# Hybrid SSD and latent-attention layer on one core: the last four FFN tiles of the down projection in parts of 352 and 224 tokens instead of 320 and 256, and the end of the issue order left to the scheduler

## The chip, the core and the metric

One NeuronCore of a Trainium2 chip. The time is the device time of one execution in microseconds; before the change three runs gave 637.97, 638.06 and 638.47, with a median of 638.06. A difference is told as a part of that median.

The engines are TensorE (PE in the profile, with its weight loads as PEld), VectorE (DVE), ScalarE (ACT), GpSimd (POOL) and SyncE (SP). Each runs its own list of instructions in order and waits on semaphores for the others. SBUF is the memory on the chip, and PSUM holds what TensorE sums, in banks of 512 f32 columns.

## What is computed

One layer for 576 tokens: 512 of a new stream and 64 of a running one. Two head groups (state space and latent attention) are mixed, and a dense SwiGLU FFN follows. The change lies in the last two lines of this part of the reference:

```python
x = x + concatenate([y_ssd, o], axis=-1) @ p['w_out']
hf = rmsnorm(x, p['norm_ffn'])
x = x + (silu(hf @ p['w_gate']) * (hf @ p['w_up'])) @ p['w_down']     # 1024 -> 2816 -> 1024
y = rmsnorm(x, norm_final)                                           # over the 1024 channels of each token
```

All inputs and outputs are f32.

## The kernel before

Channels lie on the 128 partitions and tokens along the columns, so `x` is 8 tiles of 128 x 576 (`x2[0]` to `x2[7]`, held in two buffers that the profile shows as `x2_0` for tiles 0 to 3 and `x2_1` for 4 to 7). The hidden layer of the FFN has 22 tiles of 128 channels. The first 18 go through the gate, up and down projections by a scheme of 2x2 block products with 288 columns each. Tiles 18 to 21, the last four, are gated in the same way (L894 holds the matmuls of the gate and up products, `finish` the silu and product), and their down projection is done in plain form at the very end: that is where the change is.

Products are made with three matmuls in place of one f32 matmul. Each operand is split into a rounded part and the rest, both held in the rounded f32 form (fp32r); `wh`, `wl` and the two halves of `pr18` to `pr21` are these parts, and high x high, high x low and low x high are summed in PSUM. `split_weights` (L127, L128) and `split_scaled` (L157, L159) make them. Each of the 8 output tiles needs 4 x 3 = 12 such matmuls for a part of the tokens (`down_half`, L1104).

The tokens of this last product are cut in two parts (`parts`, L1139). For part 0, tile by tile:

- 12 matmuls into a PSUM bank (`ps_l0_t`), then `add` (L1146, VectorE) adds the bank to `x2[t]`.
- ScalarE squares the sum (L1186) and multiplies the tile by its gain (`gain`, L1150); GpSimd and VectorE add the squares up (L1191, L1194, L1196).
- One f32 matmul with a matrix of ones (L1232) sums the squares over the partitions, and `norm_steps` (L186 to L193) makes the reciprocal root from it on ScalarE and VectorE, by a logarithm, an exponential and one correcting step. L1238 copies the result to SBUF for GpSimd.
- `outs` multiplies the eight tiles by it: six on VectorE (five in L1161, tile 7 in L1157), two on GpSimd (L1159). `send` (L1167) sends them to memory in pairs, on SyncE's queue.

Part 1 goes the same way, with the matmuls in `ps_l1_t`, the squares in L1240, their sums in L1245 and L1247, and its norm packed into half as many columns (L1206). Tile 7 is summed on top of a copy of `x2[7]` in PSUM (L1229). The norm is spread to all partitions by four small matmuls (L1266), and ScalarE copies it for GpSimd (L1267). The tiles are sent one by one, on SyncE's and ScalarE's queues in turn (`SENDS`, L1164). Seven matmuls (L1260), of which nothing is read, stand between L1206 and L1266.

What sets the order: the kernel is written with a scheduler that places the instructions of each engine from a simulated timeline, and `ISSUE` (L1324) is a table that overrides it. For each engine it lists the places of its instructions, counted in the order in which the program makes them, and `issue_in_order` ties each to the next one listed. An instruction that no list names is placed by the scheduler.

```python
    parts = [slice(0, 320), slice(320, T)]
    def lbank(tag, name, i):
        return bank(tag, name)[:, : parts[i].stop - parts[i].start]
    ORDERS = ((0, 4, 1, 5, 2, 3, 6, 7), (0, 2, 3, 1, 4, 5, 6, 7))
    OUTS = {3: (0, 1), 4: (2, 3, 4), 5: (5, 6), 6: (7,)}
```

Of the kernel before, what the change touches and what calls it, by code (L numbers as in the profile page):

```python
# [23 lines left out]
T = TP + TS  # L24
# [32 lines left out]
def hybrid_layer_kernel(ctx: ExitStack, tc: tile.TileContext, a, o):  # L57
# [35 lines left out]
    def tmp(name, w=T):  # L93
        return placed(tpool, [P, UPW], F32, "t", name)[:, :w]
# [1041 lines left out]

    R3 = R1
    sql = tmp("sq_last")
    parts = [slice(0, 320), slice(320, T)]  # L1139

    def lbank(tag, name, i):
        return bank(tag, name)[:, : parts[i].stop - parts[i].start]
# [298 lines left out]
4022 4019 4023-4025 4046 3969 4047-4048 4034 3989 4026-4027 4049-4050 4028 4020 3990 4029 4051 4035 4052 4036-4039  # L1441
4030-4031 3970 4032 4040-4041 4053-4054 4033 4055-4056 4042 4070 4043-4045 4021 4057-4059 4071 4060 3991 4061 4082
4062 4072-4075 4063-4065 4083 4066-4069 4076 4084 4077-4081 4085 4094-4098 4086 4099 4087 4118-4119 4100-4101 4130
4102 4106-4107 4103 4108 4131 4104 4109 4120 4088 4110-4111 4089-4090 4121 4132-4134 4091 4105 4092-4093 4187 4135
4112-4116 4136 4117 4178 4137 4122-4127 4142 4138 4128 4143-4147 4139-4140 4179 4129 4196 4148-4151 4180 4152 4181
4153 4205 4182 4154 4183 4188 4155-4156 4206 4141 4197 4157-4158 4189 4166 4159-4160 4167 4161 4190 4168-4169 4162
4238 4170 4191 4198 4163 4192 4164 4193 4171-4172 4199 4165 4184 4200 4226 4173 4201 4174-4177 4239 4194 4227 4207
4185 4208 4195 4202 4228 4203 4229 4298 4209 4230 4240-4241 4231 4186 4210 4242 4204 4211 4262 4243 4212 4214 4232
4220 4213 4217 4223 4215-4216 4233 4221 4244 4222 4218 4245 4224 4263 4250 4225 4251 4246 4252-4255 4247 4256 4219
4234 4257 4235 4248 4236 4299 4249 4264-4265 4258-4259 4237 4260-4261 4266-4267 4274-4275 4268-4269 4276 4286-4287  # L1450
4270 4288 4271-4273 4300 4289 4277-4278 4290-4294 4335 4279 4295 4323 4280 4296 4281-4282 4301 4310 4283-4285
4302-4303 4311 4304 4312 4305 4336 4297 4337 4306 4313-4315 4307-4308 4347 4338 4324-4326 4309 4327 4339-4341 4328
4316-4317 4329 4348-4349 4330 4350 4318-4321 4331 4351 4342 4332 4352 4333 4322 4353 4334 4354 4343-4346 4359
4355-4358 4360-4382 4384-4387 4383
""",
    "DVE": """
48 1 0 2-4 7 5-6 10 9 8 11 13 12 15 14 16-17 19 30 18 20 23 22 49 21 24 58 25 85 26-29 31-33 35 67 36 34 106 37 68-69
# [26 lines left out]
825 831 834 824 832 860 853 835 842 836 850 859 849 843-844 851 847 845 861 846 838 837 848 852 854 862 839 863 881  # L1484
856 866 858 855 857 864-865 868 871 885 877 867 872 878 882 874 880 873 883 876 879 890 886 891 897 889 907 875 884
888 903 909 887 910 898-899 904 911 900 892 901 919 906 915 908 912 893 914 913 869 905 920-921 923 870 922 917 894
918 924-925 916 895 928 902 927 937 926 929 896 938 932 931 939 930 933-934 940 935-936 941 943-944 942 947 945-946
949 948 950-954 956 955 958-959 957 961 963-964 967-968 971 960 962 965 969 966 970 972-978 980 979
""",
    "ACT": """  # L1490
0-5 8 6-7 11 10 9 13 12 16 14-15 19 17-18 21 20 24 23 40 22 44 25-26 52 27-31 56 32-36 50 48 41 49 60 42-43 45-46 51
# [17 lines left out]
568-569 566 564 561 567 565 571 570 572 577 574 576 575 573 578 580 579 589 582 586 588 581 587 592 590 597 585 583  # L1509
591 584 594 602-603 595 599 596 600 605 598 601 604 606 610-611 609 608 593 612 607 613 630 614 619 616 625 615 624  # L1510
621 617-618 622 626 623 620 627-629 632 631 637 633-636 640 638-639 643 645 648 646 651 654 644 649 647 656 641 650
657 655 659 658 663 660 642 661 664-665 652 666 662 674 667 669 653 675 670 668 677 676 671-673 682-685 678 680 679
688 686 690 687 689 692 697-699 695 693 700 681 701 696 691 711 703 705 707 709-710 712-715 694 706 702 704 708
716-718 720 719
""",
    "POOL": """
0-3 7 18 28 4 8 5 9 6 10 26-27 11 29 12-17 20-22 19 23-25 31 30 32-42 53 55 57 59 54 56 58 60 43-52 61-73 75 74 76-77
79 78 80-85 87 86 88-89 91 90 92-93 95 94 96-106 108-109 107 111 110
""",
    "SP": """  # L1520
11-14 16 15 18 17 19-20 22 21 25 24 39 23 37 26 40 33 38 41-43 34 44 32 45 81 46-48 57 64 79 59 58 56 62 61 65 63 60
83 70 74 67 69 68 71 78 80 88 73 75 72 66 89 77 76 82 86 90-92 87 93 100 103 101-102 104-105 109-118 120 119 122-123
121 124-130 132 131 134 133 136 135 138 137 139-144 146 145 148 147 149-150 152 151 154 153 155-156 158 157 160 159
161-169 171-172 170 174-176 173 177-178 180 179
""",
}

# [98 lines left out]
```

## Time and profile before

| what | value |
|---|---|
| median of three runs | 638.06 us |
| the profiled execution: its time / its span | 637.72 us / 635.8 us |
| PE busy in the span | 625.6 us (98%) |
| DVE, ACT, POOL busy | 552.1, 390.6, 71.6 us |
| granted TensorE clock | 0.996 |
| matmuls of L1104 with 320 columns (records, mean length) | 96, 309 ns |
| matmuls of L1104 with 256 columns | 64 at 286 ns, 32 at 282 ns |
| first part's four sends | 320 KB each, landing after 2.6 us (median) |
| second part's eight sends | 128 KB each, landing after 2.1 us (median) |

The span is the time from the first to the last instruction of the profiled execution; its own time is 1.9 us longer, and the runs' median is 0.34 us above it. A matmul's length in the profile is modelled and longer than its step, since the next one starts before it ends: what a matmul costs in a row of them is the distance from start to start. A row of the timeline has the start, the time to the last one's end, the engine, line, operation, operands and the count of those merged. A plain f32 matmul leaves two records. A row of busy time by stretches has, for each engine, the busy time and the number of instructions, then the granted clock, the DMA engines' share and GB/s.

### The profile page before, as it was taken

The page shows a single profiled execution, that of the slowest core. Times are in us where ns is not written, and L with a number is a line of the kernel's source. Part 1 is how long each engine was busy: PE and PEld are TensorE (multiplying, and loading weights), DVE is VectorE, ACT ScalarE, POOL GpSimd, SP SyncE. Part 2 cuts the span into 40 slices and gives each one's busy share as a digit, 9 for nine tenths or more (in the row PEclk, how much of TensorE's full clock was granted, in tenths as well). Part 3 has the DMA queues.
Part 4 walks back from the last instruction along what each step waited for, and adds up shares of the span by engine and source line. Part 5 has one row for each costly group of instructions (what it writes and reads, how often), then busy time and mean ns, then how long its engine had stood idle before and what let it go on. Part 6 is the DMA issues. An engine that isn't in the chain of part 4 may idle for free.

```text
span 635.8 us, 11941 instructions
## 1 busy us (share of the span) xinstructions
PE 625.6 (98%) x4631; PEld 597.7 (94%) x4631; DVE 552.1 (87%) x981; ACT 390.6 (61%) x752; POOL 71.6 (11%) x111
## 2 busy tenths in 40 slices
PE   9999999999999999999999999999999999999995
PEld 9899999985887899999999999999999999999994
DVE  6999996899867599999998997889888998999764
ACT  7655425789766479955656555656564566635464
POOL 1322122001010000000012002100111011100023
PEclk9999999999999999999999999999999999999998
DMA  9521184314131132232177436551756254733004
GB/s 309 209 59 71 35 210 152 114 30 147 72 112 35 54 133 80 85 116 67 34 185 178 120 100 145 141 136 60 187 131 163 68 162 117 164 106 134 1 1 149
DMA packets 31560, 72.66 MB, mean 114 GB/s; under 512 B 3706, under 2 KB 11400, under 8 KB 31248
## 3 DMA queue, kind: packets, MB, share of 16 engines
q1 hardware_dynamic: 25360, 60.77, 29.6%
q0 software_dynamic: 5424, 10.57, 9.3%
q8 instruction: 36, 0.59, 0.4%
q10 hardware_dynamic: 720, 0.57, 0.3%
q14 instruction: 20, 0.16, 0.1%
HBM read 58.03 MB, written 3.30 MB: 96 GB/s over the span
## 4 chain that ended last, share of the span: by engine, by line
PE 49%; issue 1%; POOL 1%; POOLq 0%; DVE 0%; ACT 0%
PE ps_x L894 17%; PE ps_dx L1034 9%; PE ps_z L894 9%; PE ps_dz L1034 5%; PE ps_y L894 4%; PE ps_l L1104 3%; PE ps_dy L1034 2%; POOL ss L1247 0%; POOL x L1159 0%; POOLq L1613 0%; PE ps_n L1232 0%; DVE x L1146 0%; ACT sq L1240 0%; POOLq L1159 0%
## 5 line engine op out<-in xcount | busy, mean ns | idle before, releaser
L894 PE MATMUL ps_x<-xop,wh_gu_S 128*128 128x288 f32 x504 | 126.3, 295 | 0.0
L894 PEld LDWEIGHTS ps_x<-xop,wh_gu_S 128*128 128x128 f32 x504 | 88.2, 188 | 0.7 <-ACT u L963 0.2
L894 PE MATMUL ps_x<-xop,wl_gu_S 128*128 128x288 f32 x252 | 73.3, 295 | 0.0
L894 PE MATMUL ps_z<-xop,gu_a 128*128 128x288 f32 x252 | 61.7, 295 | 0.0
L127 ACT CAST wh_gu_S<-gu 128x1024 fp32r<-128x1024 f32 x44 | 46.2, 1053 | 14.8 <-PE ps_y L894 4.2
L128 DVE TENSOR_TENSOR wl_gu_S<-gu,wh_gu_S 128x1024 fp32r<-128x1024 f32 x44 | 52.9, 1219 | 0.8 <-ACT wh_gu_S L127 0.5
L894 PEld LDWEIGHTS ps_x<-xop,wl_gu_S 128*128 128x128 f32 x252 | 47.1, 188 | 0.0
L1047 POOL DMA_DIRECT2D x<-db x16 | 14.9, 930 | 279.2 <-ACT db L1040 249.1
L143 PE MATMUL ps_in<-xs,wh_in 128*128 128x288 f32 x256 | 45.4, 298 | 0.0
L894 PE MATMUL ps_y<-xop,wh_gu_A 128*128 128x288 f32 x168 | 44.9, 295 | 0.0
L894 PEld LDWEIGHTS ps_z<-xop,gu_a 128*128 128x128 f32 x252 | 43.5, 188 | 0.0
L894 PE MATMUL ps_z<-xop,wh_gu_S 128*128 128x288 f32 x168 | 43.4, 295 | 0.0
L894 PE MATMUL ps_x<-xop,wh_gu_A 128*128 128x288 f32 x168 | 42.7, 295 | 0.0
L143 PEld LDWEIGHTS ps_in<-xs,wh_in 128*128 128x128 f32 x256 | 37.8, 189 | 0.2
L127 ACT CAST wh_gu_A<-gu 128x1024 fp32r<-128x1024 f32 x22 | 23.1, 1051 | 23.5 <-PE ps_x L894 16.1
L894 PEld LDWEIGHTS ps_y<-xop,wh_gu_A 128*128 128x128 f32 x168 | 30.1, 188 | 0.1
L128 DVE TENSOR_TENSOR wl_gu_A<-gu,wh_gu_A 128x1024 fp32r<-128x1024 f32 x22 | 26.8, 1220 | 3.3 <-ACT wh_gu_A L127 1.8
L894 PEld LDWEIGHTS ps_z<-xop,wh_gu_S 128*128 128x128 f32 x168 | 29.7, 188 | 0.0
L894 PEld LDWEIGHTS ps_x<-xop,wh_gu_A 128*128 128x128 f32 x168 | 29.5, 188 | 0.0
L465 PE MATMUL ps_o<-cat_y,wh_out 128*128 128x288 f32 x128 | 29.0, 312 | 0.0
L143 PE MATMUL ps_in<-xs,wl_in 128*128 128x288 f32 x128 | 27.5, 296 | 0.0
L465 PE MATMUL ps_o<-cat_o,wh_out 128*128 128x288 f32 x128 | 27.4, 297 | 0.0
(597 smaller groups left out, 2002.0 us busy)
## 6 DMA issues: line engine op xcount, KB each, us to landing
gu<-in_w_gu SPq DMA_DIRECT2D x44, 512.0 KB, 4.8
db<-in_w_down SPq DMA_DIRECT2D x16, 512.0 KB, 4.4
x<-db POOLq DMA_DIRECT2D x16, 288.0 KB, 6.6
x<-dc POOLq DMA_DIRECT2D x16, 288.0 KB, 4.3
wr_in<-in_w_in SPq DMA_DIRECT2D x8, 512.0 KB, 5.8
wr_out<-in_w_out SPq DMA_DIRECT2D x8, 512.0 KB, 3.3
cumb<-cumD SPq DMA_DIRECT2D x5, 512.0 KB, 4.9
x<-in_xT SPq DMA_DIRECT2D x2, 1152.0 KB, 5.6
```

The costliest lines, as they stand in the source:

```text
L127: act.copy(hi, raw)
L128: dve.tensor_tensor(lo, raw, hi.bitcast(F32), ALU.subtract)
L143: pe.matmul(ps[:m, hf, :n], w, x[:, hf * n : (hf + 1) * n], start=start and k == 0 and i == 0, stop=stop and k == last and i == 2,)
L465: pe.matmul(ps[:, :n], w, x[:, cols], start=not onto and k == 0 and i == 0, stop=onto or (k == len(terms) - 1 and i == 2), skip_group_chec ...
L894: pe.matmul(ps, p, q, start=not onto and first and kp == kps[0] and j == 0, stop=onto or (last and kp == kps[-1] and j == 2), skip_group_c ...
L1034: pe.matmul(ps, l, r, start=not onto and k == 0 and j == 0, stop=onto or (k == n - 1 and j == 2), skip_group_check=onto,)
L1047: pool.dma_start(x2[t], v, accum_op=ALU.add)
L1104: pe.matmul(ps, w, x[:, cols], start=first and not onto and k == 0 and i == 0, stop=onto or (last and k == len(terms) - 1 and i == 2), ski ...
```

## The change

The first part takes 352 tokens and the second 224. Everything that is cut by `parts` changes its width with it: the matmuls, sums, squares, norms, outputs and sends of the end. The number of instructions on each engine stays the same.

The second half of the change removes the end of each engine's list in `ISSUE`. The lists now stop at PE's place 4177, DVE's 940, ACT's 673, POOL's 100 and SP's 170, so that the last product, both norms and the sends are placed by the scheduler.

```diff
@@ -1136,7 +1136,7 @@
     sql = tmp("sq_last")
-    parts = [slice(0, 320), slice(320, T)]
+    parts = [slice(0, 352), slice(352, T)]
@@ -1441,17 +1441,9 @@
-4102 4106-4107 4103 4108 4131 4104 4109 4120 4088 4110-4111 4089-4090 4121 4132-4134 4091 4105 4092-4093 4187 4135
-4112-4116 4136 4117 4178 4137 4122-4127 4142 4138 4128 4143-4147 4139-4140 4179 4129 4196 4148-4151 4180 4152 4181
...
-4355-4358 4360-4382 4384-4387 4383
+4102 4106-4107 4103 4108 4131 4104 4109 4120 4088 4110-4111 4089-4090 4121 4132-4134 4091 4105 4092-4093 4135
+4112-4116 4136 4117 4137 4122-4127 4142 4138 4128 4143-4147 4139-4140 4129 4148-4156 4141 4157-4158 4166 4159-4160
+4167 4161 4168-4169 4162 4170 4163-4164 4171-4172 4165 4173-4177
 """,
     "DVE": """
...
-918 924-925 916 895 928 902 927 937 926 929 896 938 932 931 939 930 933-934 940 935-936 941 943-944 942 947 945-946
-949 948 950-954 956 955 958-959 957 961 963-964 967-968 971 960 962 965 969 966 970 972-978 980 979
+918 924-925 916 895 928 902 927 937 926 929 896 938 932 931 939 930 933-934 940 935-936
...
     "SP": """
...
-161-169 171-172 170 174-176 173 177-178 180 179
+161-169 171-172 170
```

PE, the place of the first part's norm sum (L1232), before. `ps_l1_2` is the bank of part 1, tile 2; `wh_dl1` and `wl_dl1` are the two parts of a weight tile.

```order
L1104 MATMUL ps_l1_2_7540<-pr19_7021,wh_dl1_7340 128x256
L1232 MATMUL ps_n3_0_7499<-ss3_3201,ones_86 128x320
L1104 MATMUL ps_l1_0_7504<-pr21_7328,wh_dl0_7334 128x256 x2
L1104 MATMUL ps_l1_0_7504<-pr21_7328,wl_dl0_7335 128x256
L1104 MATMUL ps_l1_2_7540<-pr19_7021,wh_dl1_7340 128x256
L1104 MATMUL ps_l1_2_7540<-pr19_7021,wl_dl1_7341 128x256
L1104 MATMUL ps_l1_3_7566<-pr18_6833,wh_dl1_7340 128x256
```

And now:

```order
L1104 MATMUL ps_l1_5_7608<-pr21_7328,wh_dl2_7346 128x224 x2
L1232 MATMUL ps_n3_0_7499<-ss3_3201,ones_86 128x352
L1104 MATMUL ps_l1_5_7608<-pr21_7328,wl_dl2_7347 128x224
L1104 MATMUL ps_l1_6_7629<-pr18_6833,wh_dl3_7352 128x224 x2
L1104 MATMUL ps_l1_6_7629<-pr18_6833,wl_dl3_7353 128x224
L1104 MATMUL ps_l1_6_7629<-pr19_7021,wh_dl3_7352 128x224 x2
L1104 MATMUL ps_l1_6_7629<-pr19_7021,wl_dl3_7353 128x224
L1104 MATMUL ps_l1_6_7629<-pr20_7245,wh_dl3_7352 128x224 x2
L1104 MATMUL ps_l1_6_7629<-pr20_7245,wl_dl3_7353 128x224
L1104 MATMUL ps_l1_6_7629<-pr21_7328,wh_dl3_7352 128x224 x2
L1104 MATMUL ps_l1_6_7629<-pr21_7328,wl_dl3_7353 128x224
```

L1232 moved from among the matmuls of part 1's first tiles to the last matmul of its tile 5. Behind it come that one, the 12 of tile 6 shown and 12 of tile 7 in the same form, then L1206.

DVE, the second norm's first step (L187 of `ps_n3_1`), before. `nr_v` and `nr_u` are the norm's working tiles, `Rp` its packed result, `sq` the squares, and `ps_r3_0` the spread result.

```order
L1157 SCALAR_TENSOR_TENSOR x2_1_2055<-x2_1_2055,par_81,ps_n3_0_7499 128x320
L1146 TENSOR_TENSOR x2_0_2053<-ps_l1_3_7566,x2_0_2053 128x256
L1146 TENSOR_TENSOR x2_1_2055<-ps_l1_4_7586,x2_1_2055 128x256
L1146 TENSOR_TENSOR x2_1_2055<-ps_l1_5_7608,x2_1_2055 128x256
L1146 TENSOR_TENSOR x2_1_2055<-ps_l1_6_7629,x2_1_2055 128x256
L1245 TENSOR_TENSOR sq_7600<-sq_7600,sq_7622 128x256
L1245 TENSOR_TENSOR sq_7600<-sq_7600,sq_7643 128x256
L187 TENSOR_SCALAR nr_v_7673<-ps_n3_1_7500 128x128
L192 TENSOR_TENSOR nr_u_7674<-nr_u_7674,nr_v_7673 128x128
```

And now:

```order
L1146 TENSOR_TENSOR x2_1_2055<-ps_l1_6_7629,x2_1_2055 128x224
L192 TENSOR_TENSOR nr_u_7503<-nr_u_7503,nr_v_7502 128x352
L193 SCALAR_TENSOR_TENSOR ps_n3_0_7499<-nr_u_7503,nr_y_7501 128x352
L1245 TENSOR_TENSOR sq_7600<-sq_7600,sq_7643 128x224
L1161 TENSOR_TENSOR x2_1_2055<-x2_1_2055,ps_n3_0_7499 128x352 x2
L1161 TENSOR_TENSOR x2_0_2053<-x2_0_2053,ps_n3_0_7499 128x352 x2
L1161 TENSOR_TENSOR x2_1_2055<-x2_1_2055,ps_n3_0_7499 128x352
L1157 SCALAR_TENSOR_TENSOR x2_1_2055<-x2_1_2055,par_81,ps_n3_0_7499 128x352
L187 TENSOR_SCALAR nr_v_7673<-ps_n3_1_7500 128x112
L192 TENSOR_TENSOR nr_u_7674<-nr_u_7674,nr_v_7673 128x112
```

The first part's last norm steps and its six outputs stood ahead of the sums of part 1's tiles 3 to 6; now they stand behind these sums, directly ahead of the second norm.

ACT, from the first norm to the end, now:

```order
L188 ACTIVATE nr_y_7501<-nr_y_7501 128x352
L1240 ACTIVATE sq_7622<-x2_1_2055 128x224
L189 ACTIVATE nr_u_7503<-nr_y_7501 128x352
L1150 ACTIVATE x2_1_2055<-x2_1_2055,par_81 128x224
L1240 ACTIVATE sq_7643<-x2_1_2055 128x224
L1150 ACTIVATE x2_1_2055<-x2_1_2055,par_81 128x224
L1238 COPY R1_99<-ps_n3_0_7499 128x352
L1240 ACTIVATE sq_7663<-ps_l1_7_7649 128x224
L186 ACTIVATE nr_y_7672<-ps_n3_1_7500 128x112
L188 ACTIVATE nr_y_7672<-nr_y_7672 128x112
L189 ACTIVATE nr_u_7674<-nr_y_7672 128x112
L1267 COPY R1_99<-ps_r3_1_7690 128x224
```

A square (L1240) now stands between L188 and L189 of the first norm, and the copy L1238 ahead of the last square. The five L1150 that stood between L189 of the second norm and L1267 have moved ahead of it.

More of the change, by code (lines that the diff above doesn't have):

```diff
@@ L1443 @@
 4062 4072-4075 4063-4065 4083 4066-4069 4076 4084 4077-4081 4085 4094-4098 4086 4099 4087 4118-4119 4100-4101 4130
-4102 4106-4107 4103 4108 4131 4104 4109 4120 4088 4110-4111 4089-4090 4121 4132-4134 4091 4105 4092-4093 4187 4135
-4112-4116 4136 4117 4178 4137 4122-4127 4142 4138 4128 4143-4147 4139-4140 4179 4129 4196 4148-4151 4180 4152 4181
[L1446 to L1453, printed above, removed]
-4355-4358 4360-4382 4384-4387 4383
+4102 4106-4107 4103 4108 4131 4104 4109 4120 4088 4110-4111 4089-4090 4121 4132-4134 4091 4105 4092-4093 4135
+4112-4116 4136 4117 4137 4122-4127 4142 4138 4128 4143-4147 4139-4140 4129 4148-4156 4141 4157-4158 4166 4159-4160
+4167 4161 4168-4169 4162 4170 4163-4164 4171-4172 4165 4173-4177
 """,
@@ L1511 @@
 621 617-618 622 626 623 620 627-629 632 631 637 633-636 640 638-639 643 645 648 646 651 654 644 649 647 656 641 650
-657 655 659 658 663 660 642 661 664-665 652 666 662 674 667 669 653 675 670 668 677 676 671-673 682-685 678 680 679
-688 686 690 687 689 692 697-699 695 693 700 681 701 696 691 711 703 705 707 709-710 712-715 694 706 702 704 708
-716-718 720 719
+657 655 659 658 663 660 642 661 664-665 652 666 662 674 667 669 653 675 670 668 677 676 671-673
 """,
@@ L1517 @@
 0-3 7 18 28 4 8 5 9 6 10 26-27 11 29 12-17 20-22 19 23-25 31 30 32-42 53 55 57 59 54 56 58 60 43-52 61-73 75 74 76-77
-79 78 80-85 87 86 88-89 91 90 92-93 95 94 96-106 108-109 107 111 110
+79 78 80-85 87 86 88-89 91 90 92-93 95 94 96-100
 """,
```

## The prediction

> **What bounds the kernel now.** I read the page first (share of each engine, then the chain that ended last), then the busy time by stretches of the end, then the timeline of that end.
>
> ```profile
> span 635.8 us, 11941 instructions
> PE 625.6 (98%) x4631; PEld 597.7 (94%) x4631; DVE 552.1 (87%) x981; ACT 390.6 (61%) x752; POOL 71.6 (11%) x111
> PE 49%; issue 1%; POOL 1%; POOLq 0%; DVE 0%; ACT 0%
> ```
>
> TensorE (PE) is busy for 98% of the span, and what else ends the chain is about 1% each. So there are two ways for an edit of the end to cost time: more TensorE time, or a longer stretch behind the last matmul, where the other engines normalise and send.
>
> ```profile
> core 0: us, PE busy (x) PEld busy (x) DVE busy (x) ACT busy (x) POOL busy (x), PEclk, DMA share, GB/s
> 615.40:620.00 4.60, 4.60 (x38) 4.44 (x37) 3.07 (x8) 3.19 (x8) 1.45 (x2) 1.00 0.01 4
> 620.00:624.50 4.50, 4.50 (x41) 4.37 (x39) 4.15 (x11) 3.19 (x9) 3.46 (x5) 1.00 0.74 255
> 624.50:628.00 3.50, 3.26 (x31) 2.77 (x31) 0.99 (x4) 2.84 (x9) 0.00 (x0) 1.00 0.13 46
> 628.00:632.00 4.00, 0.63 (x6) 0.44 (x4) 2.14 (x6) 0.82 (x3) 1.41 (x2) 0.90 0.68 222
> ```
>
> Up to 624.5 TensorE has no gap, and its clock is granted in full (1.00). From 624.5 to 625.9 the second part's norm starts, and in 624.5:628 VectorE (DVE) is nearly idle (0.99 of 3.50): whatever it had to do for the first part lies behind it. DMA is idle there too (0.13), and is then used for the second part's results alone. These two reserves are what the change touches.
>
> **TensorE's own time.** The change keeps the number of matmuls: 96 of 320 columns become 96 of 352, and 96 of 256 become 96 of 224. The price of one is the step from start to start.
>
> ```profile
> 606.53 0.60 PE L1104 MATMUL ps_l<-pr,wh_dl 128*128 128x320 f32 x3
> 606.97 0.31 PE L1104 MATMUL ps_l<-pr,wl_dl 128*128 128x320 f32 x1
> ...
> 624.04 0.40 PE L1104 MATMUL ps_l<-pr,wh_dl 128*128 128x256 f32 x2
> 624.28 0.28 PE L1104 MATMUL ps_l<-pr,wl_dl 128*128 128x256 f32 x1
> 624.49 0.33 PE L1206 MATMUL ps_n<-ss,ones 128*64 128x128 f32 x2
> ```
>
> Three of 320 columns take 606.97 - 606.53 = 0.44, so 0.147 each; two of 256 take 0.24, so 0.120. That is 0.42 ns a column, 0.107 for 256, and 0.013 on top of either. On this line 352 columns cost 0.147 + 0.013 = 0.160 and 224 cost 0.120 - 0.013 = 0.107. Sum of a pair: 0.267 before, 0.267 after; 96 pairs change nothing.
>
> But no matmul of this rounded form (fp32r) has under 256 columns in the trace, so 0.107 is an extrapolation, and I bound it. Below: a matmul with hardly any columns, whose step is its weight load.
>
> ```profile
> 123.04 1.00 PE L595 MATMUL ps_g<-ysq,ones 128*128 128x64 f32 x8
> 123.87 1.08 PE L571 MATMUL ps_s<-xw,bt 128*128 128x256 f32 x4
> ```
>
> Eight records, each with a 128x128 weight load, step over 0.83, 0.104 each: that floor lies just under 0.107. Above: the plain f32 form, which leaves two records for one instruction.
>
> ```profile
> 615.39 0.78 PE L1232 MATMUL ps_n<-ss,ones 128*128 128x320 f32 x2
> 615.77 0.64 PE L1104 MATMUL ps_l<-pr,wh_dl 128*128 128x256 f32 x2
> 616.25 0.28 PE L1104 MATMUL ps_l<-pr,wl_dl 128*128 128x256 f32 x1
> ```
>
> From 615.39 to 616.25 run one L1232 and two 256-column matmuls, so L1232 took 0.86 - 0.24 = 0.62 for 320 columns; 224 at that rate are 0.434. Between 0.104 and 0.434 I take 0.107, since 224 is only 32 columns past a row that lies on the line; the upper end becomes a rival. If the 13 ns that each step has over its columns stay on top of the weight load, a narrow one costs 0.120 as the 256-column one does, and TensorE loses 96 x 0.013 = 1.3; I keep that inside the forecast's range.
>
> A rule bears on this. The Trainium skill (TensorE: Matmul & The Clock Gate, "LDWEIGHTS (loading the stationary operand)") gives a weight load as its columns over 1.2 GHz, 107 ns for 128. By that floor the 224-column matmul is bound by its weights rather than by its columns, and anything narrower would gain nothing; the sum here would stay the same, and the row's 0.104 agrees with it.
>
> No wait enters TensorE's stream, by the new order and these prices: the narrowest cover is at the silu of the last FFN tile.
>
> ```profile
> 602.41 0.69 ACT L941 ACTIVATE g<-g 128x576 f32<-128x576 f32 x1 [4.44 <-DVE g L983]
> 603.42 0.75 DVE L942 TENSOR_TENSOR u<-u,g 128x576 f32<-128x576 f32 x1
> 604.21 0.69 ACT L157 ACTIVATE pr<-u 128x576 fp32r<-128x576 f32 x1 [1.11 <-DVE u L942]
> 604.93 0.76 DVE L159 TENSOR_TENSOR pr<-u,pr 128x576 fp32r<-128x576 f32 x1 [0.75 <-ACT pr L157]
> ```
>
> `pr21` is there about 4 us after the last gate/up matmul (L983, which waits for that, starts at 601.92; L159 ends at 605.69). The new order puts 38 wide matmuls and 2 narrow ones between it and the first that reads `pr21`: 38 x 0.160 + 2 x 0.107 = 6.3. Without that cover the price would be at most those 4 us.
>
> **The end: where the loss comes from.** The first part's norm (L1232, then L186 to L193) and its eight outputs now stand late. Before:
>
> ```profile
> 616.27 0.44 ACT L186 ACTIVATE nr_y<-ps_n 128x320 f32<-128x320 f32 x1 [1.48 <-PE ps_n L1232]
> 618.38 0.50 DVE L193 SCALAR_TENSOR_TENSOR ps_n<-nr_u,nr_y 128x320 f32<-128x320 f32 x1
> 619.08 0.42 DVE L1146 TENSOR_TENSOR x<-ps_l,x 128x256 f32<-128x256 f32 x1 [0.20 <-PE ps_l L1104]
> 619.42 2.07 DVE L1161 TENSOR_TENSOR x<-x,ps_n 128x320 f32<-128x320 f32 x5
> 621.41 0.54 DVE L1157 SCALAR_TENSOR_TENSOR x<-x,par,ps_n 128x320 f32<-128x320 f32 x1
> 624.61 0.37 ACT L1240 ACTIVATE sq<-ps_l 128x256 f32<-128x256 f32 x1
> 625.90 0.29 DVE L187 TENSOR_SCALAR nr_v<-ps_n 128x128 f32<-128x128 f32 x1 [1.28 <-ACT nr_y L186]
> 626.23 0.31 ACT L189 ACTIVATE nr_u<-nr_y 128x128 f32<-128x128 f32 x1
> 626.57 0.29 DVE L192 TENSOR_TENSOR nr_u<-nr_u,nr_v 128x128 f32<-128x128 f32 x1 [0.38 <-ACT nr_u L189]
> ```
>
> From L1232 to the end of L1157 it is 621.95 - 615.39 = 6.56, done 3.95 before the second norm's L187 at 625.90. Now only 25 narrow matmuls (1 + 12 + 12) follow L1232 before L1206. TensorE's stream is as long as before, so L1206 stands at 624.49, and L1232 starts at 624.49 - 25 x 0.107 - 0.68 (0.62 x 352/320) = 621.1. On VectorE the second L187 stands behind the whole first block, so it starts at 621.1 + 6.56 + 0.4 (twelve steps 10% wider, 0.03 to 0.04 each) + 0.4 (a square, L1240, now put between L188 and L189 on ScalarE) = 628.5, **2.6 later** than 625.90. Behind it wait L192, L193, the broadcast matmuls L1266, all eight outputs and their sends. Of the 2.6 some comes back: L192 no longer waits for L189 (0.37), and the steps are 12% narrower (112 for 128 and 224 for 256 columns; about 0.05 for an output of 0.41, some 0.5 over the chain). The last output is issued 2.6 - 0.37 - 0.5 = **1.7 later**.
>
> The five `gain` steps (L1150) that ScalarE did between L189 and L1267 now stand earlier. I cost that at nothing: L1267 waits for L1266 in either order.
>
> **The sends.** The first part's four sends are now issued while the second part is normalised, and they hold the DMA engines when its sends come.
>
> ```profile
> 621.00:622.00 1.00, 1.00 (x10) 1.00 (x9) 1.00 (x4) 0.23 (x1) 1.00 (x3) 1.00 0.75 255
> 622.00:623.00 1.00, 1.00 (x11) 1.00 (x10) 0.94 (x3) 0.68 (x2) 0.92 (x2) 1.00 1.03 358
> 630.00:631.00 1.00, 0.00 (x0) 0.00 (x0) 0.20 (x1) 0.00 (x0) 0.30 (x1) 1.00 1.07 343
> 632.00:633.00 1.00, 0.00 (x0) 0.00 (x0) 0.00 (x0) 0.00 (x0) 0.00 (x0) 0.50 0.51 168
> ...
> 620.33 10.39 SPq L1167 DMA_DIRECT2D out_yT<-x  x8
> ```
>
> Before, the first send was issued at 620.33 and data flowed from about 621.3 (255 of 358 GB/s in that microsecond), 0.95 later; the last data left at about 632.5 (busy for 0.51 of its microsecond). Now the first outputs stand at L1232 plus 4.03 (619.42 - 615.39) plus 0.6 of the corrections above, two of them take 0.95, and 0.95 to the data makes 627.6. Then 4 x 360 KB (1.44 MB at 358 GB/s) take 4.0 and 8 x 114.7 KB (0.92 MB at 343 GB/s) take 2.7: 634.4, **1.9 later** than before. The transfers are now one unbroken row, so this and not the 1.7 of the last output sets the end; with 0.1 for the turn from the one to the other, 2.0.
>
> **The sum.** TensorE 0, the late first block 2.6 of which the end keeps 1.7, the sends 2.0 in its place: the span goes from 635.8 to 637.8. The profiled execution took 637.72, 1.9 over its span, and so 639.7; the runs' median of 638.06 is 0.34 above that execution, so I forecast a median of **640.1**. The forecast's own range is 639.2 to 641.3: below, the sends overlap a little more and only half of the 1.7 is left; above, TensorE's 1.3.
>
> **The rivals.**
>
> Narrow matmuls are dear: below some width the rounded form falls back to the rate of the plain f32 form. For it: nothing in the trace shows the form under 256 columns. Against: no bend from 320 to 256, and the weight load's 0.104 does not forbid 0.107. Price: 96 x (0.434 - 0.107) = 31.4 more on TensorE, the one engine without reserve. The 25 matmuls behind L1232 would then take 10.9, the first block (6.56 + 0.8) would be done before them, and the forecast's 2.0 would go, with some 0.5 won by the narrower end: 638.1 + 31.4 - 0.5 = 669. At half that rate (0.213, each matmul doubled) it is 96 x 0.106 = 10.2, less the same: 648. Chance 0.24.
>
> The end is shorter, not longer (not slower): the first block is done before the second norm needs VectorE, and what is left is the narrower end, -0.5 from the chain and -0.1 from smaller sends: 637.5. That decides if L1232 to the end of L1157 takes less than the 25 matmuls, L1206 and its wait: 3.35 + (625.90 - 624.49) = 4.8 instead of the 7.3 I get. For it: VectorE has idle time there, and if L1232 were issued sooner than its place in the list tells, nothing else would be late. Against: TensorE and VectorE run their lists in order in every row above, and 2.5 us are far to go. Chance 0.13; in most of it the time falls between 637.5 and 639.3, in 0.05 of it below 636.8.
>
> TensorE stalls after all (a bank that VectorE frees late, since it now does the first part's sums in a row): the nearest rows are VectorE's wait of 1.28 before L187 and the 4 us of `pr21`, on top of the forecast: 641.4 to 644. The replaced order had banks free before they were needed, and VectorE is not fuller than before. Chance 0.06. That the change is not what runs is excluded: shapes and places are in the program's order above.
>
> **The numbers.** Forecast 0.57, dear narrow matmuls 0.24, shorter end 0.13, stalls 0.06. A difference of 0.2% (1.28 us) is what a measurement of this kernel can tell from none: below 636.8 is faster, above 639.3 slower. Slower: 0.57 x 0.9 + 0.24 + 0.06 = 0.81. Faster: 0.05, from the third case. Within: the rest, 0.14. The range must leave out no more than 2 in 10, so it has to reach into the dear case: from 638.6 (most of the shorter end left out) to 666 (from the doubled rate to nearly all of the f32 rate). The likeliest case's own range stays 639.2 to 641.3.
>
> **What would show it.** The step of the 224-column matmuls: 0.107 to 0.120 if I am right, 0.2 to 0.43 and a span of TensorE longer by 10 to 31 if the rival is. L1232 should start near 621.1 with 25 matmuls behind it; DVE L187 of 112 columns should start over 2 us after ScalarE's L186 of the same norm, with the L1161 steps of 352 columns between; the chain that ended last should run through DVE L1161 or the sends rather than POOL L1247; DMA should be busy without a gap from about 627.6 to the last send. I would be wrong if L1206 moves from 624.5 by more than 1.3, or if VectorE is free when the second norm's sums arrive.

## The result and the profile after

| | before | after |
|---|---|---|
| median (7 runs each) | 638.06 us (636.95 to 639.01) | 640.2 us (638.75 to 640.7) |
| ratio to the kernel before | | 1.003, 95% interval 1.0017 to 1.0043 |
| profiled execution: time / span | 637.72 / 635.8 us | 639.85 / 637.9 us |

The changed kernel is slower by 0.3%, 2.1 us. The page of its profile first: span, busy time, and the chain that ended last.

```profile
span 637.9 us, 11936 instructions
PE 626.1 (98%) x4631; PEld 598.1 (94%) x4631; DVE 551.6 (86%) x981; ACT 389.8 (61%) x752; POOL 71.3 (11%) x111
PE 89%; DVE 5%; issue 2%; DMA 1%; POOL 1%; ACT 1%; POOLq 0%; DVEq 0%; ACTq 0%
```

TensorE is busy 0.5 longer, the span is 2.1 longer. The busy time by stretches of the end (columns as before) shows where:

```profile
620.00:624.50 4.50, 4.50 (x39) 4.29 (x39) 2.32 (x6) 3.63 (x9) 1.66 (x3) 1.00 0.00 0
624.50:628.00 3.50, 2.98 (x29) 2.29 (x29) 3.02 (x8) 2.33 (x7) 1.83 (x2) 1.00 0.05 16
628.00:632.00 4.00, 1.52 (x12) 1.15 (x10) 3.07 (x11) 0.34 (x1) 0.81 (x2) 0.96 1.02 338
632.00:636.00 4.00, 0.00 (x0) 0.00 (x0) 0.26 (x1) 0.00 (x0) 0.46 (x1) 0.50 0.72 240
```

VectorE, which was nearly idle from 624.5 to 628 (0.99), is now busy there (3.02), and DMA hardly moves anything before 628 (0.05 of that stretch, at its end) and then works without a gap until the sends run out. In the timeline, TensorE's narrow matmuls and then the end:

```profile
616.46 0.39 PE L1104 MATMUL ps_l<-pr,wh_dl 128*128 128x224 f32 x2
...
617.80 0.50 PE L1104 MATMUL ps_l<-pr,wh_dl 128*128 128x224 f32 x3
...
621.37 0.77 PE L1232 MATMUL ps_n<-ss,ones 128*128 128x352 f32 x2
624.85 0.41 PE L1206 MATMUL ps_n<-ss,ones 128*64 128x112 f32 x4
625.92 2.25 DVE L1161 TENSOR_TENSOR x<-x,ps_n 128x352 f32<-128x352 f32 x5 [0.45 <-ACT R L1238]
628.08 0.57 DVE L1157 SCALAR_TENSOR_TENSOR x<-x,par,ps_n 128x352 f32<-128x352 f32 x1
628.58 0.27 DVE L187 TENSOR_SCALAR nr_v<-ps_n 128x112 f32<-128x112 f32 x1
628.95 0.28 DVE L192 TENSOR_TENSOR nr_u<-nr_u,nr_v 128x112 f32<-128x112 f32 x1
629.59 1.15 PE L1266 MATMUL ps_r<-Rp,ident 128*128 128x112 f32 x8 [1.21 <-DVE Rp L193]
630.32 1.58 DVE L1161 TENSOR_TENSOR x<-x,ps_r 128x224 f32<-128x224 f32 x5 [0.79 <-PE ps_r L1266]
631.19 1.27 POOL L1159 TENSOR_TENSOR x<-x,R 128x224 f32<-128x224 f32 x2 [3.39 <-ACT R L1267]
631.82 0.45 DVE L1157 SCALAR_TENSOR_TENSOR x<-ps_l,par,R 128x224 f32<-128x224 f32 x1
```

Between 616.46 and 617.80 start 12 matmuls (the rows between the two are left out here), so one of 224 columns steps over 0.1117. L1232 has 25 of them behind it, and the second norm's L187 stands behind the first part's last output step, L1157.

Two more views came to matter. At the end of its list each engine has a DRAIN, an instruction of its sequencer. The end of the chain, after and then before (start, length, engine and line; POOLq is GpSimd's sequencer):

```profile
631.16 0.69 POOLq L1602
631.85 0.62 POOL x L1159
```

```profile
628.86 0.76 POOLq L1613
629.62 0.69 POOL x L1159
```

And the instructions that close the program, on the last line of each (L1602, before L1613): operation, count, then shortest/median/longest in ns, then the first and the last start. After, then before:

```profile
L1602 POOLq DRAIN  x3: 46/98/5969, 631.2 to 637.6; - x3
L1602 SPq DRAIN  x3: 7/7/13, 636.1 to 637.4; - x3
```

```profile
L1613 POOLq DRAIN  x3: 46/98/6107, 628.9 to 635.5; - x3
L1613 SPq DRAIN  x3: 7/7/7, 633.5 to 635.2; - x3
```

GpSimd's first DRAIN starts at 631.16, while the last output steps are still to come, and lasts 5.97, to 637.12; its last output step had ended at 632.46 (631.19 + 1.27), 4.66 before. SyncE waits for all sends, and the second of its DRAINs, right behind that wait, is done at 636.21. In the kernel before, GpSimd's last outputs were these:

```profile
628.89 1.41 POOL L1159 TENSOR_TENSOR x<-x,R 128x256 f32<-128x256 f32 x2 [5.27 <-ACT R L1267]
```

They end at 630.30 and the drain at 634.96, again 4.66 later; SyncE is done at 633.54. In both kernels the span ends 0.79 after the later of the two, and the later is GpSimd.

### The profile page after: what moved, and what is told of

Read it like the earlier page. It is cut to its first block, busy times and chain, and to the rows that moved or that the text cites. A ratio compares the mean times of both kernels' runs of the same rounds, so it can differ in the third digit from the quotient of the medians.

```text
span 637.9 us, 11936 instructions
## 1 busy us (share of the span) xinstructions
PE 626.1 (98%) x4631; PEld 598.1 (94%) x4631; DVE 551.6 (86%) x981; ACT 389.8 (61%) x752; POOL 71.3 (11%) x111
## 4 chain that ended last, share of the span: by engine, by line
PE 89%; DVE 5%; issue 2%; DMA 1%; POOL 1%; ACT 1%; POOLq 0%; DVEq 0%; ACTq 0%
PE ps_x L894 21%; PE ps_z L894 10%; PE ps_dx L1034 9%; PE ps_in L143 8%; PE ps_o L465 7%; PE ps_y L894 5%; PE ps_dz L1034 5%; PE ps_z L465 4%; PE ps_l L1104 3%; PE ps_first L143 3%; PE ps_dy L1034 2%; PE ps_p L894 2%; PE sc L680 2%; PE pv L727 1%; PE ptp L702 1%
```

## The experiments

**How they are compared.** The way to the end of the FFN is the same code in all kernels, yet its length differs from one execution to the next: the same gate/up matmul starts between 590.07 and 592.24 in the twelve traces. So the ends are compared from that matmul, the second of the two in this row, before and after:

```profile
590.39 0.43 PE L894 MATMUL ps_z<-xop,gu_a 128*128 128x288 f32 x2
```

```profile
590.25 0.43 PE L894 MATMUL ps_z<-xop,gu_a 128*128 128x288 f32 x2
```

That is 590.53 and 590.39 (one step of 0.14 in). All times below are from this mark, each of one profiled execution; SyncE stands for the end of its DRAIN behind the wait for the sends, and what is later of it and of GpSimd's drain is in bold. The last column has the ratio to the kernel before, with its 95% interval.

| kernel | L1206 | GpSimd's last step | its drain ends | SyncE | span ends | median of the runs (before: 638.0 to 638.1) |
|---|---|---|---|---|---|---|
| before | 33.96 | 39.77 | **44.44** | 43.01 | 45.23 | 638.06 |
| after | 34.47 | 42.08 | **46.74** | 45.82 | 47.53 | 640.2 |
| split alone | 35.15 | 41.10 | **45.76** | 44.42 | 46.55 | 639.68, ratio 1.0026 (1.0015 to 1.0037) |
| order alone | 33.89 | 41.55 | **46.21** | 44.89 | 47.00 | 639.92, 1.0029 (1.0019 to 1.0039) |
| after, second norm earlier on VectorE | 34.47 | 41.71 | **46.37** | 45.69 | 47.16 | 640.09, 1.0028 (1.0015 to 1.004) |
| after, first part not sent | 34.47 | 42.08 | **46.74** | 45.61 | 47.53 | 640.63, 1.0043 (1.0028 to 1.0059) |
| after, norm earlier and a free bank | 34.47 | 40.80 | 45.46 | **45.69** | 46.46 | 639.61, 1.0033 (1.0018 to 1.0049) |
| the same, first part not sent | 34.47 | 40.79 | **45.45** | 44.94 | 46.24 | 639.7, 1.003 (1.0018 to 1.0042) |
| before, GpSimd without outputs of part 1 | 33.96 | 33.09 | 37.75 | **43.12** | 43.88 | 636.95, 0.9988 (0.9977 to 0.9999) |
| after, GpSimd without outputs of part 1 | 34.47 | 37.42 | 42.08 | **45.67** | 46.43 | 639.52, 1.0023 (1.0012 to 1.0034) |
| after, parts 384 and 192 | 35.82 | 43.13 | **47.79** | 46.38 | 48.58 | 641.46 (one run) |
| after, parts 448 and 128 | 38.67 | 45.44 | **50.10** | 48.97 | 50.88 | 643.5 (one run) |

In every row the span ends 0.76 to 0.79 after the bold number, and the drain ends 4.66 after GpSimd's last step.

From the mark the same code repeats closely: L1206 stands at 34.47 in all six kernels that have the changed kernel's order and widths up to it. The medians are coarser. They set the changed kernel, the split alone and the order alone apart from the kernel before, but the intervals of the changed kernel and of its variants overlap, so the differences among these rest on the times from the mark, one execution each.

**The split alone.** The kernel before, with its whole order, and

```diff
-    parts = [slice(0, 320), slice(320, T)]
+    parts = [slice(0, 352), slice(352, T)]
```

> Parts of 352 and 224 tokens, with every engine's order of the kernel before: the split without the new order. Theory A (the loss comes from the late first block, that is from the order): the first part's norm stands as early as before, VectorE is free when the second norm's sums come, and what is left of the change is the narrow matmul's step of 0.112 instead of 0.107 (96 x 0.0047 = +0.45 on TensorE) less the narrower end (-0.3 to -0.5): 637.9 to 638.4 us, within 0.1% of the kernel before. Rival B (the loss is the narrow matmuls', or comes with the narrower or wider parts themselves): the whole +2.1 is there again, 640.2, with L1206 as late as in the changed kernel and VectorE's second L187 late too.

Measured: a median 1.6 above the kernel before, and 1.32 more from the mark. Neither theory holds as it was put: B's late block is not there (GpSimd's last step comes 5.95 after L1206, before 5.81, after 7.61), but A's 0.1% is too little. L1206 is 1.19 late. Of that 0.5 is the matmuls' own steps (as in the changed kernel, where L1206 is 0.51 late), and most of the rest is TensorE's waits (who waits for whom, in all, times, longest):

```profile
PE ps_n L1206 <- DVE sq L1245: 0.4, 1, 0.4
PE ps_n L1206 <- POOL ss L1247: 0.2, 1, 0.2
```

TensorE waits 0.2 for a sum of squares on GpSimd before L1206, and about as long before L1232, which starts 0.35 after a matmul that steps over 0.11. Inside the norm's sum (L1206) another 0.4 goes on L1245. The listed order was made for the other widths; that wider steps in the first part and a shorter second part make the sums come too late for it fits these waits, but was not tested by an order made for this split.

**The order alone.** The changed kernel with `parts` put back.

```diff
-    parts = [slice(0, 352), slice(352, T)]
+    parts = [slice(0, 320), slice(320, T)]
```

The scheduler places the end anew for these widths, so a few steps of TensorE, VectorE and ScalarE change places against the changed kernel, and 24 matmuls instead of 25 stand between L1232 and L1206.

> Parts of 320 and 256 tokens with the code and the order of the changed kernel: the order without the split. Theory A (late first block): L1232 again has only 25 matmuls behind it, VectorE's second L187 stands behind the first block, over 2 us later than in the kernel before, and the sends run in one row to about 2 us later: 639.7 to 640.3 us, a ratio of 1.0025 to 1.0035. Rival B (narrow matmuls): no matmul is narrow, so the time is that of the kernel before, 638.0, a ratio of 1.000.

Measured: ratio 1.0029; from the mark 1.77 more than before, with L1206 where it was (33.89 and 33.96), so all of it lies behind L1206. VectorE's L187 is late without a narrow matmul in the program:

```profile
624.95 0.44 PE L1206 MATMUL ps_n<-ss,ones 128*64 128x128 f32 x4
...
628.49 0.29 DVE L187 TENSOR_SCALAR nr_v<-ps_n 128x128 f32<-128x128 f32 x1
```

3.54 from the one to the other; in the changed kernel 3.73, in the kernel before 1.41. So the late first block is the order's, and it is worth 1.8. The two parts don't add up (1.32 + 1.77 against 2.30). Most of the difference of 0.79 is TensorE's waits ahead of the norm, which the split has under the old order and not under the new one: L1206 stands at 35.15 there and at 34.47 in the changed kernel, 0.68 earlier.

**The second norm earlier on VectorE.** In the changed kernel the lists of TensorE, VectorE and ScalarE are written out to the end. Those of TensorE and ScalarE keep the order that the scheduler had made; in VectorE's, L187, L192 and L193 stand among the first part's outputs. VectorE's order at this place, as a diff:

```diff
+L1161 x2
+L187
+L1161
+L192
+L193
 L1161 x2
-L1161 x3
 L1157
-L187
-L192
-L193
```

> The changed kernel, with one thing moved on VectorE: the second norm's three steps (L187, L192, L193) stand between the first part's output steps instead of behind the last of them. Theory A1 (the unbroken row of sends sets the end, the late L187 alone does not): L187 starts near 627.0 instead of 628.6, the broadcast L1266 1.1 earlier, but the last byte leaves as late as before the move, since the first part's sends hold the DMA engines: 640.0 to 640.3 us, a ratio of 0.9995 to 1.000 against the changed kernel. Rival A2 (VectorE's queue ahead of L187 sets the end): the end comes 0.7 to 1.1 earlier with L187: 639.1 to 639.5 us.

Measured: 640.09, and 0.37 less than the changed kernel from the mark. The time is about A1's, and its reason is wrong. L187 moved as expected, yet the second broadcast pair did not:

```profile
626.71 0.28 DVE L187 TENSOR_SCALAR nr_v<-ps_n 128x112 f32<-128x112 f32 x1 [0.16 <-ACT nr_y L186]
...
629.35 0.70 PE L1266 MATMUL ps_r<-Rp,ident 128*128 128x112 f32 x4 [0.66 <-DVE x L1157]
...
630.51 1.27 POOL L1159 TENSOR_TENSOR x<-x,R 128x224 f32<-128x224 f32 x2 [3.02 <-ACT R L1267]
```

That pair writes the PSUM bank that holds the first norm until L1157 has read it. Behind the pair wait L1267 and GpSimd's two outputs, and these come 0.37 earlier, as much as the end.

**The first part is not sent.** The changed kernel without its first four sends.

```diff
-        if i == 0 and t ^ 1 in sent[i]:
+        if False and i == 0 and t ^ 1 in sent[i]:
```

> The changed kernel without the four sends of the first part (352 of 576 tokens of yT are computed and not written out), all else as it was. Theory A1 (two limits that stand close: the row of sends, 2.0 later than in the kernel before, and the last output, 1.7 later): DMA is idle until the second part's sends, but the last output is as late as ever, and the end comes only 0.2 to 0.5 earlier: 639.7 to 640.0 us. Rival A3 (the sends alone cost the 2 us, by contention): the end comes back to that of the kernel before, 638.0 us or less.

Measured: from the mark the same end as with the sends, 47.53, although DMA was idle until the second part's results came:

```profile
628.00:630.00 2.00, 1.15 (x11) 0.96 (x9) 1.90 (x6) 0.33 (x2) 0.58 (x1) 1.00 0.00 0
630.00:632.00 2.00, 1.15 (x8) 0.97 (x8) 1.18 (x5) 0.35 (x1) 0.03 (x1) 1.00 0.00 0
632.00:634.00 2.00, 0.00 (x0) 0.00 (x0) 1.04 (x4) 0.00 (x0) 1.25 (x2) 0.82 0.84 282
```

A3 falls, and so does A1 by its 0.2 to 0.5: the row of sends did not set the end at all. It hardly held up the second part's sends either: without the first four SyncE is done only 0.21 earlier (45.61 against 45.82), and still 2.60 later than in the kernel before (43.01). (The median is 0.4 higher than the changed kernel's; the mark lies 0.8 later in this trace.) In the six profiles so far the span ended some 5.45 after the last output step, and the next pair tested that.

**A free bank for the broadcast.** As two experiments above, with the last bank of `ps_r3` moved to one that tile 1 had left:

```diff
-02102120212012012012012012012012010210201210210210210212102102120120120120120121021021020210210221
+02102120212012012012012012012012010210201210210210210212102102120120120120120121021021020210210220
```

> The changed kernel with VectorE's three steps of the second norm between the first part's outputs (as in the run before it), and the second broadcast pair in a PSUM bank that is free, so that it need not wait for the first part's last output (L1157). All times from a common mark, the start of the same gate/up matmul some 34 us ahead of L1206. Theory O (the last output sets the end: in the six kernels profiled so far the span ends 5.42 to 5.50 after the last output step): the last output comes 0.8 to 1.0 earlier than in the changed kernel, and the end with it: 46.5 to 46.8 from the mark instead of 47.5, a median near 639.3. Rival S (the unbroken row of sends sets the end): the sends start as before, the last output is 0.8 to 1.0 earlier, and the end moves by no more than 0.3.

and the same without the first four sends:

> The kernel of the run before without the first part's four sends (352 of 576 tokens of yT are not written out). Theory O: the same end as with them, 46.5 to 46.8 from the mark, 5.45 after the last output. Rival S: the end comes 0.5 or more earlier than with the sends, because nothing holds the DMA engines when the second part's results come.

Measured: 46.46 and 46.24. The first is about O's (0.04 under its range), 1.07 better than the changed kernel, with a row of sends that ends nearly as late as there (45.69 and 45.82); S falls. The second is 0.26 below O's range: without the sends the end is 0.22 earlier, so sends did count in the first. GpSimd's outputs and then the closing instructions of the first tell why:

```profile
630.04 1.27 POOL L1159 TENSOR_TENSOR x<-x,R 128x224 f32<-128x224 f32 x2 [2.12 <-ACT R L1267]
```

```profile
L1609 POOLq DRAIN  x3: 46/98/5967, 630.0 to 636.7; - x3
L1609 SPq DRAIN  x3: 7/7/13, 636.1 to 636.4; - x3
```

GpSimd's last step ends at 631.31, its drain at 635.97 (630.0 + 5.97); SyncE is done at 636.20. Here the sends are last, by 0.23. Without them GpSimd is last again (45.45 against 44.94). VectorE's last output ended at 41.07 from the mark in both, and the end did not follow it. So what fits is not the last output step on any engine, but GpSimd's, through its drain, or the sends where they are later; that is theory D of the next pair.

**No output of part 1 on GpSimd.** The kernel before with

```diff
-    SENDS = ((2, sp), (3, act), (4, sp), (5, act), (0, sp), (6, act), (7, sp), (1, act))
+    SENDS = ((0, sp), (2, act), (3, sp), (1, act), (4, sp), (5, act), (6, sp), (7, act))
-    POOLS = ((0, 1), (0, 1))
+    POOLS = ((0, 1), ())
```

and its lists of the last outputs and sends in the order in which they are made:

> The kernel before, with the second part's outputs of tiles 0 and 1 computed on VectorE instead of GpSimd, and the eight sends listed in the order in which VectorE then finishes them. Theory D (the end is GpSimd's closing drain, which in the ten kernels profiled so far ends 4.66 after GpSimd's last output step; SyncE, which waits for the sends, is done at 633.5 in the kernel before, 1.4 earlier than the drain at 635.0): GpSimd's last step is now one of the first part's, its drain is long over, SyncE's wait for the sends sets the end. VectorE's two more steps (0.33 each) put the last output at about 630.9, SyncE is done at 633.8 or so and the span ends 0.8 later: 44.0 to 44.6 from the mark instead of 45.27, a median of 636.9 to 637.4, faster than both kernels. Rival O (the end follows the last output step on whatever engine by 5.45): the last output is 0.6 later, and so is the end: 638.6.

and the changed kernel with the same two lines:

> The changed kernel with the same edit: no output of the second part on GpSimd. Theory D: GpSimd's drain (637.13 in the changed kernel) no longer ends last; SyncE's wait for the sends does, which ended at 636.2 there and is put off by 0.1 to 0.4 by the later last output, and by the row of sends: 46.7 to 47.1 from the mark instead of 47.51, a median of 639.4 to 639.8. Rival O: the last output is 0.4 to 0.6 later and so is the end: 640.6 to 640.8.

Measured: 43.88 and 46.43 from the mark, medians of 636.95 and 639.52. Both medians are D's, and O (638.6 and 640.6 or more) falls; from the mark both ends come earlier than D's ranges, by 0.1 and 0.3. VectorE's last outputs and the closing instructions of the first of them:

```profile
627.91 2.41 DVE L1161 TENSOR_TENSOR x<-x,ps_r 128x256 f32<-128x256 f32 x7 [0.87 <-PE ps_r L1266]
630.23 0.48 DVE L1157 SCALAR_TENSOR_TENSOR x<-ps_l,par,R 128x256 f32<-128x256 f32 x1
```

```profile
L1613 POOLq DRAIN  x3: 46/98/5426, 622.7 to 634.0; - x3
L1613 SPq DRAIN  x3: 7/7/13, 633.4 to 633.7; - x3
```

VectorE's last output is 0.67 later from the mark (40.34 against 39.67), and the span ends 1.35 earlier: GpSimd's drain is over at 628.1, and SyncE, done at 633.49, ends the program. The new order of the sends is not what gained: from the mark SyncE is 0.11 later than in the kernel before. By its median it is the fastest of these kernels, 0.12% ahead of the kernel before (0.01% to 0.23%).

**Other widths.** The changed kernel with parts of 384 and 192, and of 448 and 128.

> The changed kernel with parts of 384 and 192 tokens, the order made by the same code. Floor theory (below some 240 columns a matmul is bound by its weight load): the step of the 192-column matmuls is the 224-column one's, 0.112, those of 384 columns cost 0.173, and mark to L1206 is 34.46 + 96 x 0.013 = 35.7. Linear theory (the step keeps 0.42 ns a column): 0.093, and mark to L1206 34.0 to 34.5.

> The changed kernel with parts of 448 and 128 tokens. Floor theory: the 128-column step is 0.112 again, the 448-column one 0.200, and mark to L1206 is 34.46 + 96 x 0.040 = 38.3. Linear theory: 0.067 and 0.200, mark to L1206 34.0 to 34.5. Third possibility (the rounded form is dear below some width): a step of 0.2 or more, mark to L1206 above 42.

Measured: mark to L1206 35.82 and 38.67, 0.1 and 0.4 above the floor theory's 35.7 and 38.3 and outside the ranges of the other theories. The rows, of 192 and then of 128 columns:

```profile
620.33 0.38 PE L1104 MATMUL ps_l<-pr,wh_dl 128*128 128x192 f32 x2
...
621.33 0.27 PE L1104 MATMUL ps_l<-pr,wh_dl 128*128 128x192 f32 x1
```

```profile
620.11 0.39 PE L1104 MATMUL ps_l<-pr,wh_dl 128*128 128x128 f32 x2
...
621.11 0.39 PE L1104 MATMUL ps_l<-pr,wh_dl 128*128 128x128 f32 x2
```

Nine matmuls start in 1.00 each time: 0.111, as with 224 columns. The Trainium skill (TensorE: Matmul & The Clock Gate, "LDWEIGHTS (loading the stationary operand)") gives a formula for a weight load, by which one of 128 columns is an estimated 107 ns. The traces agree that the step stops falling near there, at 0.111 to 0.112; that it is the weight load which holds it there is the reading that fits, and no run here changed the weight load alone.

## Why the prediction was right, and where it was not

The forecast case came true, and its number (640.1 against 640.2). One step of it was wrong and one term too small, and that the number fits so well is partly luck.

**TensorE's time.** Put at 0, with 0.107 for the 224-column matmul off the line of the wider ones. It stepped over 0.1117: the line ends at a floor, above the 0.104 of the row that the prediction took as its lower bound. The term is 96 x 0.0047 = 0.45, and L1206 was 0.51 later from the mark. The upper price of 0.120 in the range covered it. No bank and no `pr21` was waited for, as forecast; dear narrow matmuls are excluded down to 128 columns. TensorE does wait inside the norm's sum (L1206), 0.3 for VectorE's L1245 and 0.3 for ScalarE's L1240, which the forecast did not have. It cost nothing here: ScalarE's L188 ends at 627.26, and L187 starts at 628.58, held up by VectorE's outputs.

**The late first block.** Right. L1232 started at 621.37 (forecast 621.1), L187 at 628.58 (628.5), behind the whole block, and L192 had no wait. Counted from L1206, L187 is 2.3 late instead of 2.6 (3.73 against 1.41). The last output was to be 1.7 later: from L1206 VectorE's is 1.70 later and GpSimd's last step 1.80, so of the delay 0.5 to 0.6 came back and not 0.9, and these two misses cancel. The order alone gives 1.85 for GpSimd's last step, and moving L187 forward with a free bank takes back 1.28 of the 1.80. Shown.

**The sends.** The row was there as forecast, unbroken from about 627.8 to 634.6 (forecast 627.6 to 634.4). The step that failed is the sentence after it: "so this and not the 1.7 of the last output sets the end". Without the first part's sends the end stood where it was, and the second part's sends were done only 0.21 earlier, so the idea that the first sends hold the DMA engines against the second ones accounts for little of it. What sets the end in both kernels is GpSimd's drain, 4.66 behind its last output step, 0.92 later than the sends in the changed kernel and 1.43 in the kernel before. The 2.0 for the sends should have been 1.8 for GpSimd's last step; with TensorE's 0.5 that is 2.3, less 0.14 for a front that happened to be shorter in the profiled execution: 2.17, the difference of the two spans (637.92 - 635.75). The forecast had 2.0: it left out the 0.5 and put the sends' 2.0 where GpSimd's 1.8 belongs.

**The signs.** Step, L1232, L187 and the row of sends were as named. The chain was not: it was to run through DVE L1161 or the sends, and ended in GpSimd's L1159 and its sequencer, as the chain of the kernel before had done. That line was quoted in the prediction ("POOL 1%; POOLq 0%"), and I read it as small shares and did not ask which instruction ended last.

**Not settled.** Why the way to the mark differs by up to 2.2 us between executions was not tried. The split alone was read from its waits; an order made for it was not tried. What GpSimd's drain does in its 4.66 us is open; the runs show only that it takes them, and that the end moves when they no longer come last.

## What to carry to other kernels

Look at the closing instructions of every engine, and at when each is done: an engine with little to do can still end the program. The last steps of the chain of waits, however small their share, say where to begin, but they are not the answer. In the kernel with the norm earlier and a free bank the chain ends so:

```profile
631.22 0.36 DVE x L1157
```

VectorE has the last output step there, yet the program waits for the sends (636.20) and GpSimd's drain (635.97) is next. In the kernel before, GpSimd's two last output steps saved VectorE 0.67 at the very end and cost the program 1.35; work for it belongs where its drain has time to pass. And an issue order belongs to its tile widths: here each of the two, moved without the other, cost 1.3 to 1.8. So compare ends from a common mark close by, where a difference of 0.2% can be taken apart.

## What the runs showed of the hardware

GpSimd's closing drain ended 4.66 us after its last tensor step in all twelve traces, whether that step was 352, 256, 224, 192 or 128 columns wide; VectorE's ended 0.05 after its own last step. The rounded f32 matmul with a 128x128 weight load steps over 0.111 to 0.112 at 224, 192 and 128 columns alike, and 0.120 at 256; on the line of 0.42 ns a column through the wider ones 224 columns would take 0.107, so the bend lies between 224 and 256 columns.
